# Seven half-width products of a matmul pair, with the upper and lower operand streamed in one 512-column matmul, and the lower parts of the down weights made by an accumulating transfer

## The chip, the core and the metric

The kernel runs on one core of a Trainium2 chip. The metric is the device time of one execution in microseconds, as the median of several runs. Before the change it was 2463.43 us (three runs, 2463.13 to 2463.51). In the text PE is the matmul engine (TensorE), PEld its weight loads, DVE the vector engine, ACT the scalar engine, POOL the GpSimd engine and SP the engine that issues most transfers. Every engine works through its own instructions in the order in which the program wrote them.

## The reference

Two transformer blocks on a sequence of 512 tokens with 1024 features, all in float32. What matters here are the five feed-forward networks, which hold most of the work:

```
x = x + jnp.square(jax.nn.relu(h2 @ w_up[l])) @ w_down[l]             # block 1, 4096 hidden features
...
def swiglu(h, w_gate, w_up, w_down):
    return (jax.nn.silu(h @ w_gate) * (h @ w_up)) @ w_down            # block 2, 2816 hidden, four times
```

Attention, a short convolution and the projections stand between them; the change does not touch those.

## The kernel before

**Upper and lower parts.** The fast matmul mode (float32r) keeps fewer bits than float32. So each operand is split in two: an upper part, rounded by a copy on ACT (`h`, tile `wh` for a weight), and a lower part, the rest, subtracted by DVE (`lo`, tile `wl`). A product of weights and activations is the sum of three matmuls: upper by upper, upper weights by lower activations, lower weights by upper activations. In the code these are lines 1082 to 1084, and lines 450 to 452 for ordinary tiles.

**Seven products for eight.** The weights of a hidden row come in pairs (gate and up, or two neighbouring rows of `w_up`). For most pairs the 2 by 2 block product over (weight halves, token halves) is done in the Strassen-Winograd way, with seven products of 256 columns rather than eight. `product(m, p)` does product `p` of pair `m`; `PRODUCTS = (1, 2, 6, 7, 5, 4, 3)` is the order. Each product is four K chunks by three matmuls of 256 columns. Products 1, 6, 5 and 3 accumulate one after another in the left half of a PSUM bank `X`, products 2, then 7 and 4 in the left half of a bank `YZ`; after each product ACT or DVE reads the running sum into the tiles `g` and `u`. The weight sums that products 6, 7, 5 and 3 need (`s1` to `s4`) are made by DVE in `combine` (line 355). There are 98 such pairs. The first pair or two of a network are done by `plain`, with ordinary matmuls of 512 columns.

**Stages.** `ffn_order` writes the order by hand. The hidden rows are cut in slices (four slices of 4, 6, 5 and 7 pairs in the networks of block 2, six slices in block 1). Stage 0 has the products of slice 0, after the plain pairs. Stage s holds the products of slice s and, between them, the down projection (`down`, tiles `..._D`) of slice s-1, cut in 16 items of two to four K chunks by three matmuls of 512 columns. A tail of down items of the last slice ends the network. In this text (0, ffn2) is the second network of layer 0 of block 2, and so on; `mlp` is the network of block 1.

**Weights ahead of their use.** Weights are loaded by SP in units of up to 512 KB (`raw`, five buffers) in the order of use. `split_item` (line 357) prepares one item, that is one product's or one down item's weights: ACT casts `wh` (line 376), `combine` makes the sums that the next item needs, DVE subtracts to get `wl` (line 378). `split_to` keeps five items (AHEAD) prepared beyond the one that PE works on, in a ring of seven buffers. In the written order the reading out of product i stands ahead of the preparing of item i+5, on ACT and on DVE.

**After the seventh product** `finish_relu` or `finish_silu` scales and activates `g` and `u`, and the result is split again for the down projection.

Of the kernel before, what the change touches and what calls it, by code (L numbers as in the profile page):

```python
# [231 lines left out]
def two_blocks(ctx, tc, plan, xT, wstream, vecs, sinks, rpb_g, dists, masks, outT):  # L232
# [76 lines left out]
    for i in range(4):  # L309
        s = slot[7 * i:7 * i + 7]  # L310
        lo, hi = slice(0, H), slice(H, S)
        xs.append({"b11": (s[0][:, lo], s[1][:, lo]), "t1": (s[0][:, hi], s[1][:, hi]),
                   "b21": (s[2][:, lo], s[3][:, lo]), "b22": (s[2][:, hi], s[3][:, hi]),
                   "t2": (s[4][:, lo], s[5][:, lo]), "t3": (s[4][:, hi], s[5][:, hi]),
                   "t4": (s[6][:, lo], s[6][:, hi]), "slots": s})
# [41 lines left out]
    def split_item(idx):  # L357
# [19 lines left out]
        combine(idx + 1)  # L377
        nc.vector.tensor_tensor(lo[:, :w], src, h[:, :w].bitcast(F32), ALU.subtract)  # L378
# [681 lines left out]
    def feed_forward(name, slices, pairs, start, finish, scale, prepare):  # L1060
# [6 lines left out]
        def product(m, p):  # L1067
# [363 lines left out]
```

## Time and profile before

| | |
|---|---|
| median of three runs | 2463.43 us |
| the profiled execution | 2464.76 us, span 2463.0 us |
| PE busy | 2436.1 us (99%), 15098 matmuls |
| DVE busy | 1960.7 us (80%) |
| ACT busy | 1261.0 us (51%) |
| POOL busy | 24.6 us (1%) |
| granted PE clock, mean | 0.996 (of 2.4 GHz) |

The span runs from the first to the last instruction. Busy time is the union of an engine's instructions. A matmul's duration holds its way through the array, so matmuls of one stream overlap in the records and their cost is read from start to start. The same goes, to a smaller degree, for DVE: when its instructions follow each other without a pause, each starts about 0.08 us before the one ahead of it is recorded as ended.

### The profile page before, as it was taken

Reading aid. Unit: us, or ns where it says so; the run is one execution under the profiler, and the core shown is the slowest. Engines: PE = TensorE matmul, PEld = TensorE weight load, DVE = VectorE, ACT = ScalarE, POOL = GpSimd, SP = SyncE. Lnnn points to the kernel's source line nnn. Section 1 sums busy time; section 2 is a strip of 40 time slices with the busy share of each in tenths; the row PEclk is TensorE's granted clock in tenths of the full one; section 3 lists DMA queues with packets and bytes.
Section 4 is the critical chain, followed back from the end, with each engine's and each line's share of the span. In section 5 each row is a group of like instructions: output and inputs, shape, how many; then the busy total and the mean of one; then the engine's idle time right before and its main releaser. Section 6 shows DMA issues by size and latency. Waiting matters only on the chain.

```text
span 2463.0 us, 39488 instructions
## 1 busy us (share of the span) xinstructions
PE 2436.1 (99%) x15098; PEld 2167.0 (88%) x15098; DVE 1960.7 (80%) x3943; ACT 1261.0 (51%) x2744; POOL 24.6 (1%) x37
## 2 busy tenths in 40 slices
PE   8999999999999999999999999999999999999998
PEld 6888888999879999988899999899999878999997
DVE  7778678877679878768798888898887687988885
ACT  5554355544455545544565445665445455654454
POOL 2000000000000000000000000000000000000000
PEclk9999999999999999999999999999999999999999
DMA  4222432233322332332223323323333322233332
GB/s 161 69 92 88 118 114 82 94 101 100 106 85 91 101 115 88 114 95 69 84 80 103 107 99 101 102 93 112 98 104 106 102 69 77 75 107 108 106 94 79
DMA packets 73901, 239.45 MB, mean 97 GB/s; under 512 B 8320, under 2 KB 10384, under 8 KB 73712
## 3 DMA queue, kind: packets, MB, share of 16 engines
q1 hardware_dynamic: 70496, 228.10, 29.0%
q0 software_dynamic: 1776, 7.27, 1.0%
q8 instruction: 118, 1.93, 0.3%
q10 hardware_dynamic: 1440, 1.57, 0.2%
q14 instruction: 71, 0.58, 0.1%
HBM read 234.81 MB, written 2.10 MB: 96 GB/s over the span
## 4 chain that ended last, share of the span: by engine, by line
PE 93%; DVE 5%; ACT 1%; issue 0%; DMA 0%; SPq 0%; DVEq 0%; ACTq 0%
PE X L1084 7%; PE X L1083 7%; PE X L1082 7%; PE YZ L1082 5%; PE YZ L1083 5%; PE YZ L1084 5%; PE mlp_D L451 2%; PE mlp_D L450 2%; PE mlp_D L452 2%; PE 0, 'ffn2'_D L450 2%; PE 1, 'ffn1'_D L450 2%; PE 0, 'ffn1'_D L450 2%; PE 0, 'ffn1'_D L451 2%; PE 0, 'ffn2'_D L451 2%; PE 1, 'ffn1'_D L451 2%; PE 0, 'ffn1'_D L452 2%
## 5 line engine op out<-in xcount | busy, mean ns | idle before, releaser
L378 DVE TENSOR_TENSOR wl<-raw,wh 128x512 fp32r<-128x512 f32 (+2 forms) x890 | 531.7, 609 | 98.3 <-ACT wh L376 91.4
L376 ACT CAST wh<-raw 128x512 fp32r<-128x512 f32 (+2 forms) x890 | 469.6, 555 | 8.4 <-DMA raw<-in_w 2.6
L1082 PE MATMUL X<-r,wh 128*128 128x256 f32 x1568 | 445.2, 284 | 3.8 <-ACT g L1088 3.6
L1084 PE MATMUL X<-r,wl 128*128 128x256 f32 x1568 | 444.0, 283 | 0.0
L1083 PE MATMUL X<-r,wh 128*128 128x256 f32 x1568 | 443.9, 283 | 0.0
L376 ACT CAST wh<-s 128x512 fp32r<-128x512 f32 x392 | 242.7, 620 | 224.6 <-DVE s L355 219.2
L1082 PE MATMUL YZ<-r,wh 128*128 128x256 f32 x1176 | 334.4, 284 | 0.8 <-ACT u L1094 0.8
L1083 PE MATMUL YZ<-r,wh 128*128 128x256 f32 x1176 | 333.3, 283 | 0.0
L1084 PE MATMUL YZ<-r,wl 128*128 128x256 f32 x1176 | 333.2, 283 | 0.0
L378 DVE TENSOR_TENSOR wl<-s,wh 128x512 fp32r<-128x512 f32 x392 | 268.8, 686 | 69.5 <-ACT wh L376 67.6
L1082 PEld LDWEIGHTS X<-r,wh 128*128 128x128 f32 x1568 | 300.1, 191 | 15.2 <-ACT g L1088 4.0
L1083 PEld LDWEIGHTS X<-r,wh 128*128 128x128 f32 x1568 | 300.1, 191 | 10.3 <-issue 1.2
L1084 PEld LDWEIGHTS X<-r,wl 128*128 128x128 f32 x1568 | 300.2, 191 | 0.0
L1082 PEld LDWEIGHTS YZ<-r,wh 128*128 128x128 f32 x1176 | 226.3, 192 | 1.6 <-ACT u L1094 1.4
L1083 PEld LDWEIGHTS YZ<-r,wh 128*128 128x128 f32 x1176 | 226.3, 192 | 0.2 <-issue 0.2
L1084 PEld LDWEIGHTS YZ<-r,wl 128*128 128x128 f32 x1176 | 226.3, 192 | 0.0
L1096 ACT COPY g<-X 128x256 f32<-128x256 f32 x98 | 36.5, 372 | 141.6 <-PE X L1084 141.5
L1097 DVE TENSOR_TENSOR u<-u,g 128x256 f32<-128x256 f32 x98 | 41.6, 424 | 75.8 <-ACT g L1096 75.8
L450 PE MATMUL mlp_D<-r,wh 128*128 128x512 f32 x256 | 100.1, 391 | 0.0
L451 PE MATMUL mlp_D<-r,wh 128*128 128x512 f32 x256 | 100.1, 391 | 0.0
L452 PE MATMUL mlp_D<-r,wl 128*128 128x512 f32 x256 | 99.6, 389 | 0.0
L1092 ACT COPY u<-X 128x256 f32<-128x256 f32 x98 | 36.5, 373 | 101.0 <-PE X L1084 101.0
(429 smaller groups left out, 5258.9 us busy)
## 6 DMA issues: line engine op xcount, KB each, us to landing
raw<-in_w SPq DMA_DIRECT2D x320, 512.0 KB, 3.7
raw<-in_w SPq DMA_DIRECT2D x64, 384.0 KB, 3.5
raw<-in_w SPq DMA_DIRECT2D x32, 448.0 KB, 3.5
raw<-in_w SPq DMA_DIRECT2D x32, 320.0 KB, 2.9
raw<-in_w SPq DMA_DIRECT2D x28, 256.0 KB, 2.6
bb<-in_rpb POOLq DMA_DIRECT2D x12, 384.0 KB, 3.3
xt<-in_x POOLq DMA_DIRECT2D x8, 256.0 KB, 2.9
xt<-in_x SPq DMA_DIRECT2D x1, 1024.0 KB, 12.7
```

The costliest lines, as they stand in the source:

```text
L376: nc.scalar.copy(h[:, :w], src)
L378: nc.vector.tensor_tensor(lo[:, :w], src, h[:, :w].bitcast(F32), ALU.subtract)
L450: nc.tensor.matmul(self.ps, h[:, c], hx, start=(self.n == 1), stop=False)
L451: nc.tensor.matmul(self.ps, h[:, c], lx, start=False, stop=False)
L452: nc.tensor.matmul(self.ps, lo[:, c], hx, start=False, stop=end)
L1082: nc.tensor.matmul(out, h[:, c], hx, start=first, stop=False, skip_group_check=skip)
L1083: nc.tensor.matmul(out, h[:, c], lx, start=False, stop=False, skip_group_check=skip)
L1084: nc.tensor.matmul(out, l[:, c], hx, start=False, stop=(k == 3), skip_group_check=skip)
L1092: nc.scalar.copy(u[:, lo], out)
L1096: nc.scalar.copy(g[:, hi], out)
L1097: nc.vector.tensor_tensor(u[:, hi], u[:, hi], g[:, hi], ALU.add)
```

## The change

The upper and the lower activations of a product come to stand so that one access pattern covers both: the 28 slots of 512 columns that hold them are one tile, `xall`, and the upper and the lower quarter of a product's operand lie a fixed step apart in it. Per K chunk one matmul streams 512 columns [upper, lower] against the upper weights and writes both halves of the bank; a second one streams the 256 upper columns against the lower weights into the left half. So the bank holds two partial sums, and the reading out adds them: both halves are copied or read, and more additions are done on DVE. Product 3, whose sum the finishing step read from the bank, is now read out into `g` first, and the finishing step takes `g` as one operand of 512 columns.

For down weights (`key[1:2] == ("D",)`) the lower part is no longer subtracted by DVE. ACT writes the negated upper part into `wl`, and a transfer issued by POOL adds the raw weights to it in place.

```
+    xall = cst.tile([P, 28 * S], F32R, name="xall")
...
         nc.scalar.copy(h[:, :w], src)
-        combine(idx + 1)
-        nc.vector.tensor_tensor(lo[:, :w], src, h[:, :w].bitcast(F32), ALU.subtract)
+        if key[1:2] == ("D",):
+            nc.scalar.activation(lo[:, :w], h[:, :w].bitcast(F32), AF.Copy, scale=-1.0)
+            nc.gpsimd.dma_start(lo[:, :w].bitcast(F32), src, accum_op=ALU.add)
+            combine(idx + 1)
+        else:
+            combine(idx + 1)
+            nc.vector.tensor_tensor(lo[:, :w], src, h[:, :w].bitcast(F32), ALU.subtract)
...
-                nc.tensor.matmul(out, h[:, c], hx, start=first, stop=False, skip_group_check=skip)
-                nc.tensor.matmul(out, h[:, c], lx, start=False, stop=False, skip_group_check=skip)
-                nc.tensor.matmul(out, l[:, c], hx, start=False, stop=(k == 3), skip_group_check=skip)
+                if end:
+                    nc.tensor.matmul(out, l[:, c], hx, start=False, stop=False, skip_group_check=True)
+                nc.tensor.matmul(both, h[:, c], hlx, start=first, stop=end, skip_group_check=True)
+                if not end:
+                    nc.tensor.matmul(out, l[:, c], hx, start=False, stop=False, skip_group_check=True)
             done(idx)
             g, u = d["g"], d["u"]
-            if p == 1:
-                nc.scalar.copy(g[:, lo], out)
-            elif p == 2:
-                nc.vector.tensor_tensor(g[:, lo], out, g[:, lo], ALU.add)
-            elif p == 6:
-                nc.scalar.copy(u[:, lo], out)
+            if p in (2, 4):
+                t = g if p == 2 else u
+                nc.vector.tensor_tensor(t[:, lo], out, t[:, lo], ALU.add)
+                nc.vector.tensor_tensor(t[:, lo], low, t[:, lo], ALU.add)
+            elif p in (1, 6):
+                t = g if p == 1 else u
+                nc.scalar.copy(t, d["X"])
+                nc.vector.tensor_tensor(t[:, lo], t[:, lo], t[:, hi], ALU.add)
             elif p == 7:
                 nc.scalar.copy(u[:, hi], out)
-            elif p == 5:
-                nc.scalar.copy(g[:, hi], out)
+                nc.scalar.copy(g[:, hi], low)
                 nc.vector.tensor_tensor(u[:, hi], u[:, hi], g[:, hi], ALU.add)
-            elif p == 4:
-                nc.vector.tensor_tensor(u[:, lo], out, u[:, lo], ALU.add)
             else:
-                later.extend(finish(m, g, u, out, hid))
+                t = g[:, hi]
+                nc.scalar.copy(t, out)
+                nc.vector.tensor_tensor(t, low, t, ALU.add)
+                if p == 5:
+                    nc.vector.tensor_tensor(u[:, hi], u[:, hi], g[:, hi], ALU.add)
+            if p == 3:
+                later.extend(finish(m, g, u, hid))
                 held.pop(m)
...
-            nc.vector.tensor_tensor(g[:, hi], c12, inv[:, hi], ALU.mult)
-            nc.vector.tensor_tensor(g[:, lo], g[:, lo], inv[:, lo], ALU.mult)
+    def finish_silu(m, g, u, hid):
+        nc.vector.tensor_tensor(g, g, inv, ALU.mult)
```

DVE first, in stage 2 of (0, ffn1) before the change: what stands in its queue from the reading out of product 5 of a pair to that pair's finishing step. `wl` are lower weight parts, `s` the weight sums, a name in brackets is the engine that is waited for.

```order
L1097 TENSOR_TENSOR u_9480<-u_9480,g_9479 128x256 [waits Activation_49]
L378 TENSOR_TENSOR wl_9606<-raw_9386,wh_9605 128x512 [waits PE_49,Activation_49]
L1099 TENSOR_TENSOR u_9480<-YZ_9553,u_9480 128x256 [waits PE_49]
L355 TENSOR_TENSOR s_444_9625<-raw_9441 128x512 [waits DMAHW5_49]
L355 TENSOR_TENSOR s_444_9627<-s_444_9625,raw_9386 128x512 [waits DVE_49]
L378 TENSOR_TENSOR wl_9623<-raw_9571,wh_9622 128x384 [waits DMAHW6_49,Activation_49]
L355 TENSOR_TENSOR s_445_9633<-raw_9386,raw_9441 128x512
L378 TENSOR_TENSOR wl_9631<-s_444_9627,wh_9630 128x512 [waits Activation_49]
L897 SCALAR_TENSOR_TENSOR xt<-0, 'ffn1'_D_5_9577,xt 128x512 [waits PE_49]
L1272 TENSOR_TENSOR g_9479<-X_9478,inv 128x256 [waits PE_49]
L1273 TENSOR_TENSOR g_9479<-g_9479,inv 128x256
L1274 TENSOR_TENSOR u_9480<-u_9480,inv 128x512
```

The same part of DVE's queue for a pair of that network with the change.

```order
L1118 TENSOR_TENSOR g_9563<-X_9562,g_9563 128x256 [waits Activation_49]
L1120 TENSOR_TENSOR u_9564<-u_9564,g_9563 128x256 [waits DVE_49]
L391 TENSOR_TENSOR wl_9660<-raw_9481,wh_9659 128x512 [waits Activation_49]
L1105 TENSOR_TENSOR u_9564<-YZ_9632,u_9564 128x256 [waits PE_49]
L1106 TENSOR_TENSOR u_9564<-YZ_9632,u_9564 128x256 [waits DVE_49]
L362 TENSOR_TENSOR s_473_9678<-raw_9483 128x512 [waits DMAHW7_49]
L362 TENSOR_TENSOR s_473_9680<-s_473_9678,raw_9481 128x512 [waits DVE_49]
L362 TENSOR_TENSOR s_474_9685<-raw_9481,raw_9483 128x512
L391 TENSOR_TENSOR wl_9683<-s_473_9680,wh_9682 128x512 [waits Activation_49]
L910 SCALAR_TENSOR_TENSOR xt<-0, 'ffn1'_D_1_9596,xt 128x512 [waits PE_49]
L1118 TENSOR_TENSOR g_9563<-X_9562,g_9563 128x256 [waits Activation_49]
L1284 TENSOR_TENSOR g_9563<-g_9563,inv 128x512 [waits DVE_49]
```

The down item's subtraction (128x384) is gone; products 5, 4 and 3 have one more addition each, and three of the added or widened instructions wait for the one just ahead of them on DVE.

PE, before: the start of product 3 of a pair, which accumulates in `X` after product 5.

```order
L1082 MATMUL X_9478<-r_90,wh_9567 128x256 [waits Activation_49]
L1083 MATMUL X_9478<-r_91,wh_9567 128x256
L1084 MATMUL X_9478<-r_90,wl_9568 128x256
L1082 MATMUL X_9478<-r_97,wh_9567 128x256
L1083 MATMUL X_9478<-r_98,wh_9567 128x256
L1084 MATMUL X_9478<-r_97,wl_9568 128x256
```

PE, with the change: the end of a down item of three K chunks, and then the start of product 3 of a pair.

```order
L465 MATMUL 0, 'ffn1'_D_4_9021<-r_7186,wl_8943 128x512
L1098 MATMUL X_8881<-xall,wh_8961 128x512 [waits DVE_49]
L1100 MATMUL X_8881<-xall,wl_8962 128x256
L1098 MATMUL X_8881<-xall,wh_8961 128x512
L1100 MATMUL X_8881<-xall,wl_8962 128x256
L1098 MATMUL X_8881<-xall,wh_8961 128x512
```

Three matmuls of 256 columns have become one of 512 and one of 256; and product 3 now waits for DVE, which reads product 5's lower half out of the bank, where it waited for ACT alone.

ACT, with the change, in stage 3 of (0, ffn1): around a down item, whose `wl` is written by the second of its two rows and added to by a transfer.

```order
L1117 COPY g_9867<-X_9866 128x256 [waits PE_49]
L383 CAST wh_10025<-raw_9780 128x384
L386 ACTIVATE wl_10026<-wh_10025 128x384 [waits DMASW4_49,Activation_49]
L1109 COPY g_10033<-X_10032 128x512 [waits PE_49]
L1290 ACTIVATE g_9867<-g_9867 128x512 [waits DVE_49]
```

Between the cast and PE's use of `wl` there now stand an ACT instruction, a POOL instruction and a transfer, where there was one DVE instruction.

## Rows read from the trace of the kernel before

**Rows 1.** The page: busy time by engine, and the chain that ended last.
```profile
PE 2436.1 (99%) x15098; PEld 2167.0 (88%) x15098; DVE 1960.7 (80%) x3943; ACT 1261.0 (51%) x2744; POOL 24.6 (1%) x37
PE 93%; DVE 5%; ACT 1%; issue 0%; DMA 0%; SPq 0%; DVEq 0%; ACTq 0%
```

**Rows 2.** Timeline of PE (start us, us long): a product, then a down item.
```profile
1366.96 0.28 PE L1082 MATMUL YZ<-r,wh 128*128 128x256 f32 x1
...
1368.29 0.28 PE L1084 MATMUL YZ<-r,wl 128*128 128x256 f32 x1
1368.41 0.40 PE L450 MATMUL 0, 'ffn2'_D<-r,wh 128*128 128x512 f32 x1
...
1370.47 0.28 PE L1082 MATMUL X<-r,wh 128*128 128x256 f32 x1
```

**Rows 3.** Busy us by window: stages 0 to 3 of (0, ffn2).
```profile
1250.50:1283.00 32.50, 32.26 (x264) 31.55 (x263) 31.27 (x59) 21.18 (x42) 0.00 (x0) 1.00 0.26 90
1283.00:1365.50 82.50, 82.50 (x602) 78.39 (x601) 73.47 (x140) 44.55 (x95) 0.00 (x0) 1.00 0.32 103
1365.50:1448.90 83.40, 83.40 (x567) 77.44 (x566) 67.23 (x122) 39.59 (x82) 0.00 (x0) 1.00 0.31 102
1448.90:1546.90 98.00, 98.00 (x710) 92.96 (x709) 83.16 (x154) 51.36 (x108) 0.00 (x0) 1.00 0.33 105
```

**Rows 4.** The same view: stages 0 and 1 of (0, ffn1).
```profile
736.40:763.50 27.10, 23.74 (x172) 22.38 (x171) 26.62 (x47) 15.20 (x31) 0.00 (x0) 0.94 0.21 68
763.50:846.10 82.60, 82.60 (x603) 78.49 (x602) 74.38 (x142) 44.63 (x96) 0.00 (x0) 1.00 0.33 103
```

**Rows 5.** Timeline of DVE in stage 0 of (0, ffn2).
```profile
1274.40 0.41 DVE L1272 TENSOR_TENSOR g<-X,inv 128x256 f32<-128x256 f32 x1
1274.74 0.41 DVE L1273 TENSOR_TENSOR g<-g,inv 128x256 f32<-128x256 f32 x1
1275.07 0.68 DVE L1274 TENSOR_TENSOR u<-u,inv 128x512 f32<-128x512 f32 x1
1275.67 0.68 DVE L378 TENSOR_TENSOR wl<-s,wh 128x512 fp32r<-128x512 f32 x1
...
1280.39 0.68 DVE L355 TENSOR_TENSOR s<-raw 128x512 f32<-128x512 f32 x1
1281.11 0.69 DVE L355 TENSOR_TENSOR s<-s,raw 128x512 f32<-128x512 f32 x1
```

**Rows 6.** Groups by line and shape: DVE's subtractions of 256 and 384 columns.
```profile
L378 DVE TENSOR_TENSOR wl<-raw,wh 128x384 fp32r<-128x384 f32 x192 | 105.3, 553 | 32.3 <-ACT wh L376 32.3
L378 DVE TENSOR_TENSOR wl<-raw,wh 128x256 fp32r<-128x256 f32 x160 | 66.3, 418 | 11.0 <-ACT wh L376 10.5
```

**Rows 7.** Windows: the third product stage of the `mlp` network.
```profile
430.73:482.91 52.18, 52.18 (x351) 48.22 (x350) 42.41 (x81) 27.28 (x61) 0.00 (x0) 1.00 0.31 99
```

**Rows 8.** Timeline of ACT: the cast of a down item's weights.
```profile
1288.93 0.40 ACT L376 CAST wh<-raw 128x256 fp32r<-128x256 f32 x1
1289.24 0.36 ACT L1094 COPY u<-YZ 128x256 f32<-128x256 f32 x1
```

**Rows 9.** Timeline of PE: the first use of the same item's weights.
```profile
1292.99 0.40 PE L450 MATMUL 0, 'ffn2'_D<-r,wh 128*128 128x512 f32 x1
...
1293.45 0.39 PE L452 MATMUL 0, 'ffn2'_D<-r,wl 128*128 128x512 f32 x1
```

**Rows 10.** The page, transfers: count, KB each, median us from issue to landing.
```profile
bb<-in_rpb POOLq DMA_DIRECT2D x12, 384.0 KB, 3.3
xt<-in_x POOLq DMA_DIRECT2D x8, 256.0 KB, 2.9
...
out<-xt ACTq DMA_DIRECT2D x8, 128.0 KB, 1.8
...
dst<-in_dist POOLq DMA_DIRECT2D x1, 320.0 KB, 8.8
```

**Rows 11.** The page's groups: casts of weights, idle time before them, and what ended it.
```profile
L376 ACT CAST wh<-raw 128x512 fp32r<-128x512 f32 (+2 forms) x890 | 469.6, 555 | 8.4 <-DMA raw<-in_w 2.6
```

More of the change, by code (lines that the diff above doesn't have):

```diff
@@ L251, in two_blocks @@
     whole, slot = [None] * 52, [None] * 52
+    xall = cst.tile([P, 28 * S], F32R, name="xall")
     def use_slot(i, dtype):
+        if i < 28:
+            assert dtype == F32R
+            whole[i] = slot[i] = xall[:, S * i:S * i + S]
+            return slot[i]
         whole[i] = slot_p.tile([P, S if i < 50 else 768], dtype, tag=f"r{i}", name=f"r{i}")
@@ L310, in two_blocks @@
         s = slot[7 * i:7 * i + 7]
[L311 to L315, printed above, removed]
+        quarters = xall[:, 7 * i * S:7 * i * S + 7 * S].rearrange("p (a q) -> p a q", q=H)
+        xs.append({name: (quarters[:, k:k + step + 1:step, :], quarters[:, k, :])
+                   for name, k, step in (("b11", 0, 2), ("t1", 1, 2), ("b21", 4, 2), ("b22", 5, 2),
+                                         ("t2", 8, 2), ("t3", 9, 2), ("t4", 12, 1))})
+        xs[i]["slots"] = s
     st = {"unit": 0, "split": 0, "next": 0, "off": 0}
@@ L1072, in product @@
             if p in (2, 7):
-                d["YZ"] = bank(f"YZ{m}")[:, :H]
-            out = d["YZ"] if p in (2, 7, 4) else d["X"][:, :H]
+                d["YZ"] = bank(f"YZ{m}")
+            both = d["YZ"] if p in (2, 7, 4) else d["X"]
+            out, low = both[:, :H], both[:, H:]
+            both = both.rearrange("p (a q) -> p a q", a=2)
             idx = item(key, p, 0)
@@ L1077, in product @@
             for k in range(4):
-                hx, lx = xs[k][A_OF[p]]
+                hlx, hx = xs[k][A_OF[p]]
                 c = slice(P * k, P * k + P)
-                first = k == 0 and p in (1, 2, 7)
-                skip = p not in (1, 2, 7)
-                nc.tensor.matmul(out, h[:, c], hx, start=first, stop=False, skip_group_check=skip)
-                nc.tensor.matmul(out, h[:, c], lx, start=False, stop=False, skip_group_check=skip)
-                nc.tensor.matmul(out, l[:, c], hx, start=False, stop=(k == 3), skip_group_check=skip)
+                first, end = k == 0 and p in (1, 2, 7), k == 3
@@ L1131, in plain_end @@
             (_, t0, i0), (_, t1, i1) = held.pop(m)
-            later.extend(finish(m, t0, t1, None, hid))
+            later.extend(finish(m, t0, t1, hid))
             later.append(lambda: give(i0 + i1))
@@ L1249, in feed_forward, with finish_relu @@
         return first, rest
-    def finish_relu(m, g, u, c12, hid):
-        lo, hi = slice(0, H), slice(H, S)
-        if c12 is None:
-            nc.vector.scalar_tensor_tensor(g, g, 0.0, inv, ALU.max, ALU.mult)
-        else:
-            nc.vector.scalar_tensor_tensor(g[:, hi], c12, 0.0, inv[:, hi], ALU.max, ALU.mult)
-            nc.vector.scalar_tensor_tensor(g[:, lo], g[:, lo], 0.0, inv[:, lo], ALU.max, ALU.mult)
+    def finish_relu(m, g, u, hid):
+        nc.vector.scalar_tensor_tensor(g, g, 0.0, inv, ALU.max, ALU.mult)
         nc.vector.scalar_tensor_tensor(u, u, 0.0, inv, ALU.max, ALU.mult)
@@ L1265, in finish_relu @@
         return [lambda: split(m, g), lambda: split(m + 1, u)]
-    def finish_silu(m, g, u, c12, hid):
-        lo, hi = slice(0, H), slice(H, S)
-        if c12 is None:
-            nc.vector.tensor_tensor(g, g, inv, ALU.mult)
-        else:
-            nc.vector.tensor_tensor(g[:, hi], c12, inv[:, hi], ALU.mult)
-            nc.vector.tensor_tensor(g[:, lo], g[:, lo], inv[:, lo], ALU.mult)
+    def finish_silu(m, g, u, hid):
+        nc.vector.tensor_tensor(g, g, inv, ALU.mult)
         nc.vector.tensor_tensor(u, u, inv, ALU.mult)
```

## The prediction

> **What bounds the kernel now.** I read four views in this order. First the page: PE is busy 99% of the span and holds 93% of the chain that ended last, while DVE is busy 80% and ACT 51% [rows 1]. So PE is the bound on the whole, and DVE is the engine with the least to spare. Second the timeline of PE, for the price of a matmul from start to start: the twelve 256-column matmuls of a product take 1368.41 - 1366.96 = 1.45 us, 0.120 us each, and the nine 512-column ones of a down item 1370.47 - 1368.41 = 2.06 us, 0.229 us each. A 256-column one behind a 512-column one and a 512-column one behind a 256-column one go at the same prices, by the width of the one ahead [rows 2]. Third, windows laid on the stages of one network, since 80% is a mean: DVE is busy 31.27 of 32.50 us in stage 0 (96%), 73.47 of 82.50 in stage 1 (89%), 67.23 of 83.40 in stage 2 (81%), 83.16 of 98.00 in stage 3 (85%) [rows 3]. In (0, ffn1) stage 0 has 26.62 of 27.10 [rows 4]. Stage 0 has products alone, and there DVE is a second bound already. Fourth DVE's own timeline in that stage: its rows follow without a pause, so the step from start to start is the price: 0.34 us for 256 columns, 0.60 for 512, and 0.72 where the next instruction needs the result of this one (1280.39 to 1281.11), 0.12 more [rows 5].
>
> **The change, part by part.**
>
> *Matmuls.* A K chunk cost 3 x 0.120 = 0.360 us and will cost 0.229 + 0.120 = 0.349 us. There are 98 pairs x 7 products x 4 chunks = 2744 chunks, so 2744 x 0.011 = 30 us of PE time go, 0.31 us per pair. A third of the weight loads of these products goes with them, but the loads lie beside the matmuls (PEld is busy 88% under PE's 99% [rows 1]). This is the largest gain that the change can have. A price for 512 columns split in two runs of 256 in memory is not in the trace; the nearest rows bound the chunk by 0.349 and, if two runs cost as two matmuls, 0.360. I take the first.
>
> Against the row stands a rule of the Trainium skill, "TensorE: Matmul & The Clock Gate", section "Back-to-back issue gap": at full clock a matmul takes its columns divided by 2.4 GHz plus about 2.5 ns, so merging two would save 2.5 ns, an estimate of 6.9 us over 2744 chunks and not 30. The trace does not agree with it here: the rule gives 109 ns and 216 ns where the rows have 120 and 229.
>
> *Reading out, on DVE.* Gone per pair are five 256-column instructions (L1090, L1097, L1099, L1272, L1273). New are ten of 256 columns and one of 512: two each for products 2 and 4, one each for 1, 6, 7 and 3, two for 5, and the finishing step on `g` at full width. That is 5 x 0.334 + 0.60 = 2.27 us more. Four of them wait for the instruction ahead of them on DVE (the second additions of 2 and 4, the one behind product 5's, the finishing step behind product 3's): 4 x 0.12 = 0.48 us. Together 2.75 us per pair, 270 us over 98 pairs. If the waits cost nothing it is 2.27.
>
> *Down weights, off DVE.* Each of the 352 down items drops one subtraction: 0.34 us at 256 columns, 0.47 at 384 (the means of 418 and 553 ns less the overlap of 0.08 us, 0.68 against a step of 0.60), 0.60 at 512 [rows 5, 6]. Of these items 128 have 256 columns, 192 have 384 and 32 have 512, by the code: 128 x 0.34 + 192 x 0.47 + 32 x 0.60 = 153 us, but they fall in stages 1 to 3 and the tails. None falls in stage 0.
>
> *By stage.* For (0, ffn2), which the two networks of layer 1 resemble, stages 0 and 1 have three and six pairs and stage 1 has 16 down items of 256 columns. DVE: 31.27 + 73.47 - 16 x 0.34 + 9 x 2.75 = 124.1 us, where the two stages take 115.0 us now and PE would need 115.0 - 9 x 0.31 = 112.2. DVE becomes the bound. How far may it lag? Weights are prepared five items ahead, but product 3 starts when DVE has read product 5's lower half out of the same bank, and in stage 0 only product 4 (1.4 us) stands between. So I give DVE 1 us of lag, and the two stages take 123 us: 8 us more. (0, ffn1) has two pairs in stage 0: 26.62 + 74.38 - 5.4 + 8 x 2.75 = 117.6 us against 109.7, less the same 1 us: 7 more. Over the four networks 3 x 8 + 7 = 31 us lost.
> Stage 2 holds 16 down items of 384 columns: DVE 67.23 - 16 x 0.47 + 5 x 2.75 = 73.5 us against PE's 83.4 - 5 x 0.31 = 81.9. PE bounds: 1.5 us gained, 6 over four networks.
> Stage 3 holds eight of 256 and eight of 384 columns: DVE 83.16 - 8 x 0.34 - 8 x 0.47 + 7 x 2.75 = 95.9 us, PE 98.0 - 7 x 0.31 = 95.8. A tie; two queues that wait on each other lose a little, so 97 and 1 us gained, 4 over four networks.
> `mlp` has many down items to a pair: DVE 42.41 of 52.18 us for three pairs [rows 7], and 42.41 + 3 x 2.75 - 16 x 0.34 = 45.2 stays under PE's 51. Fifteen pairs gain 15 x 0.31 = 4.6; its one pair without down items has 2.75 us more on DVE, of which the lag takes most, and loses about 1: 3.6 gained.
>
> *Down weights, by ACT and the transfer.* ACT gets 352 negations of some 0.4 us (the nearest rows are its cast and copy of 256 columns, 0.40 and 0.36 [rows 8]) and wider copies. It is busy 21.18 of 32.50 us at most [rows 3], so throughput is no issue; latency is. The item of stage 1 with the shortest notice is cast at 1288.93, its `wh` is used at 1292.99 and its `wl` first at 1293.45: 4.5 us [rows 8, 9]. The new way takes the cast 0.40, a negation of 0.40, and a transfer from POOL. No row shows an accumulating transfer. POOL's plain ones land after 2.9 us for 256 KB and 3.3 for 384; the shortest of any is 1.8 and the longest of POOL's 8.8, in the first microseconds beside the opening loads [rows 10]. Most down items move 128 or 192 KB. I take 2.9, the nearest row: 0.4 + 0.4 + 0.1 + 2.9 = 3.8 us, within 4.5, cost nothing. At 1.8 it is nothing too; at 8.8 it would be late by some 5 us on each of the 272 items that lie between products. The cover is gone at a landing of about 3.6 us. Behind a late `wl` stands all of PE's queue. On POOL nothing else is queued in these networks. On SP the load that refills a `raw` buffer now waits for the transfer that reads it, some 3 us later than for DVE; casts waited 2.6 us in all for loads [rows 11], and five buffers are ahead, so this costs nothing as long as a buffer's turn (about 4 us for 512 KB of weights) times five exceeds the load and the added 3 us.
>
> *Sum.* 31 - 6 - 4 - 3.6 = +17 us on the profiled execution's 2464.76 us, 1.3 us over the median of the runs. On the median: 2481 us.
>
> **The rivals.** *DVE's additions hide and PE's gain stays.* DVE is 80% busy over the span [rows 1], some 500 us free for a net 117 of new work (270 - 153), and five prepared items are 7 us of lead. If the lag is allowed to be that, if no own wait costs anything (9 x 2.27 rather than 9 x 2.75), stages 0 and 1 come to 119.8 - 5 = 115 us, even with now, and stages 2 and 3 give 1.5 + 2.2 each: 4 x 3.7 + 3.6 = 18 us gained, 2445 us; with everything hidden 2433. Against it: DVE runs without a pause through stage 0 already [rows 5], and the wait in front of product 3 cuts the lead. It decides if DVE's work in stages 0 and 1 stays under about 116 us.
> *The transfers are late.* If adding in place doubles what a transfer does, a landing near 4.5 us, the short-notice items are late by up to 1 us. With 272 items between products, a third to a half of them late, and a part of it under DVE's own lag, that is 50 us: 2530 us. For it: nothing in the trace shows that kind of transfer, and the raw loads keep the transfer engines 32% busy [rows 3]. Against: the size is below that of the 2.9 us row.
> *Merging saves less.* With 2.5 ns a chunk in place of 11, stages 2 and 3 and `mlp` lose their gain, 13.6 us down to about 1: 2494 us. The rule of the skill's page on TensorE named above would have it so.
> That the change does not do what it says I rule out: 2744 matmuls are gone from PE's queue, and the attention and projection stages keep their waits, though 28 slots are one tile.
>
> **How the numbers follow.** DVE-bound stages 0 and 1, as summed: 0.52, from 2460 to 2508 (3% of idle DVE time in stages 0, 1 and 3 would add 27 us to 2481; 2.27 a pair takes 16 from it and a little more lag the rest). Hidden additions: 0.20, 2433 to 2458. Late transfers: 0.23, 2490 and far up. Merging that saves little: 0.05. The predicted time is 2481 us. The range 2448 to 2530 leaves out about half of the second case and a third of the third. A measurement of this kernel tells 0.2% from no change, about 5 us: faster 0.20, the same 0.08 (the near end of the first case), slower 0.72.
>
> **What would show it.** PE: in products, steps of 0.229 and 0.120 us. DVE busy near 100% in stages 0 and 1 of the block 2 networks and about 98% in stage 3, with PE idle in front of product 3 put down to DVE's reading of `X`; stage 0 of (0, ffn2) near 39 us and stage 1 near 84; stage 2 near 82 and set by PE. Transfers from POOL landing under 3.6 us, and no idle PE in front of a down item's third matmul. I am wrong if PE waits there on transfers, or if stages 0 and 1 together come to 115 us or less.

## The result, and the profile after

The changed kernel takes 2660.38 us (median of four runs, 2651.63 to 2665.0), the kernel before 2463.47 (2463.13 to 2464.25) beside it. The ratio is 1.0795, with a 95% interval of 1.0766 to 1.0823: 197 us slower, where 17 were forecast. The direction was right, the size was not, and the time lies outside the range.

The profiled execution took 2651.63 us, with a span of 2649.9 us and a mean granted clock of 0.980 (0.996 before). These lines of its page answer to [rows 1, 10]: busy times, the software queue, the chain, and the transfers of `wl` (count, KB each, median us to landing).

```profile
PE 2486.7 (94%) x12354; PEld 2038.7 (77%) x12354; DVE 2074.7 (78%) x4179; ACT 1524.8 (58%) x3292; POOL 332.4 (13%) x389
...
q0 software_dynamic: 52464, 70.20, 15.9%
...
PE 56%; DMA 14%; issue 14%; DVE 12%; ACT 4%; POOL 1%; POOLq 0%; SPq 0%; DVEq 0%; ACTq 0%
...
wl<-raw POOLq DMA_DIRECT2D x192, 192.0 KB, 3.9
...
wl<-raw POOLq DMA_DIRECT2D x128, 128.0 KB, 2.8
...
wl<-raw POOLq DMA_DIRECT2D x32, 256.0 KB, 5.1
```

DMA held 0% of the chain before; now 14% of the span is chained to it, and 13% is `DMA wl<-raw` alone. DVE's share of the span fell from 80 to 78%, so the kernel is not simply DVE-bound. The medians of landing are 2.8 to 5.1 us, where the prediction took 2.9 for all. The median hides the worse part: over the 352 transfers a tenth land after 6.3 us or later, the latest after 7.8.

Who stands still is in the waits of PE over the whole span (us in total, times, the longest):

```profile
PE 0, 'ffn2'_D L465 <- DMA wl<-raw: 23.1, 13, 3.4
PE 1, 'ffn2'_D L465 <- DMA wl<-raw: 22.2, 14, 3.8
PE mlp_D L465 <- DMA wl<-raw: 21.6, 21, 3.1
PE 1, 'ffn1'_D L465 <- DMA wl<-raw: 19.6, 12, 3.7
PE 0, 'ffn1'_D L465 <- DMA wl<-raw: 18.9, 11, 3.4
```

L465 is the third matmul of a down item, the first that reads `wl`. It waits 71 times, 105.4 us in all. One of these waits on PE's timeline, in stage 2 of (0, ffn2), with the merged products ahead of it; the first three lines answer to [rows 2]:

```profile
1463.82 0.40 PE L1098 MATMUL X<-xall,wh 128*128 128x512 f32 x1
1464.06 0.28 PE L1100 MATMUL X<-xall,wl 128*128 128x256 f32 x1
1464.18 0.40 PE L1098 MATMUL X<-xall,wh 128*128 128x512 f32 x1
...
1466.86 0.40 PE L464 MATMUL 0, 'ffn2'_D<-r,wh 128*128 128x512 f32 x1
1469.77 0.50 PE L465 MATMUL 0, 'ffn2'_D<-r,wl 128*128 128x512 f32 x1 [2.51 <-DMA wl<-raw]
...
1472.09 0.63 PE L1098 MATMUL X<-xall,wh 128*128 128x512 f32 x1
1472.51 0.41 PE L1100 MATMUL X<-xall,wl 128*128 128x256 f32 x1
1472.72 0.63 PE L1098 MATMUL X<-xall,wh 128*128 128x512 f32 x1
```

A chunk takes 1464.18 - 1463.82 = 0.36 us before the wait and 1472.72 - 1472.09 = 0.63 after it. PE idled 2.5 us, and about 1 us after it resumed the clock dropped to the lower level (1.2 GHz), for 3.4 us. So this wait is paid twice. It is not so for all: behind 14 of the 71 waits, 1.9 to 3.8 us long, the clock fell within 1.5 us after PE had resumed, each time for 3.4 us; behind the other 57, 0.2 to 3.7 us long, it did not. The granted clock sums it up, as an estimate: (1 - 0.980) x 2650 = 53 us of PE's speed lost, against (1 - 0.996) x 2463 = 10 before. Of the 53 us, 14 x 3.4 / 2 = 24 lie right behind such waits.

Why was this transfer late? POOL's timeline, and the transfers of the stretch from 1462 to 1470 us (issues, KB, median us to landing):

```profile
1462.66 0.87 POOL L387 DMA_DIRECT2D wl<-raw  x1 [2.74 <-ACT wl L386]
```

```profile
raw<-in_w SPq DMA_DIRECT2D x2, 512.0 KB, 4.9
raw<-in_w SPq DMA_DIRECT2D x1, 384.0 KB, 4.5
wl<-raw POOLq DMA_DIRECT2D x2, 192.0 KB, 5.1
```

Three loads of raw weights were issued from 1462.20 to 1463.10 us, around the transfer's issue at 1462.66. It landed after 7.1 us; the one issued at 1467.59, when most of these loads were done, after 3.1.

The windows of (0, ffn2) answer to [rows 3] (busy us of PE, PEld, DVE, ACT, POOL with counts; clock, DMA share, GB/s):

```profile
1320.29:1360.55 40.26, 33.05 (x179) 26.82 (x178) 39.20 (x76) 24.17 (x48) 0.00 (x0) 1.00 0.20 72
1360.55:1454.05 93.50, 86.66 (x433) 72.43 (x432) 83.34 (x159) 56.02 (x123) 14.83 (x17) 0.95 0.45 113
1454.05:1544.86 90.81, 85.08 (x425) 70.61 (x424) 74.09 (x138) 52.20 (x107) 13.08 (x15) 0.98 0.51 128
1544.86:1658.43 113.57, 102.56 (x514) 85.68 (x513) 93.34 (x176) 66.79 (x141) 17.44 (x20) 0.95 0.45 113
```

Two different losses. Stage 0 has no transfer and grew from 32.5 to 40.3 us with DVE busy 97%: that one was forecast (near 39). Stages 1 to 3 grew by 11, 7 and 16 us with DVE at 82 to 89% and the clock under 1: that one was not. In stage 0 PE waits for the reading out, and for nothing else:

```profile
PE X L1098 <- DVE g L1118: 2.4, 2, 1.4
PE X L1098 <- ACT u L1109: 2.1, 2, 1.4
PE YZ L1098 <- ACT g L1113: 1.8, 2, 0.9
PE X L1098 <- ACT g L1109: 0.9, 1, 0.9
```

### The profile page after: what moved, and what is told of

It reads as the page before. It is cut to its first block, busy times and chain, and to the rows that moved or that the text cites. A ratio compares the mean times of both kernels' runs of the same rounds, so it can differ in the third digit from the quotient of the medians.

```text
span 2649.9 us, 35945 instructions
## 1 busy us (share of the span) xinstructions
PE 2486.7 (94%) x12354; PEld 2038.7 (77%) x12354; DVE 2074.7 (78%) x4179; ACT 1524.8 (58%) x3292; POOL 332.4 (13%) x389
## 4 chain that ended last, share of the span: by engine, by line
PE 56%; DMA 14%; issue 14%; DVE 12%; ACT 4%; POOL 1%; POOLq 0%; SPq 0%; DVEq 0%; ACTq 0%
DMA wl<-raw 13%; PE X L1098 6%; PE YZ L1098 3%; DVE wl L391 3%; PE X L1100 2%; DVE s L362 2%; PE 0, 'ffn1'_D L465 1%; PE 1, 'ffn1'_D L465 1%; PE 0, 'ffn2'_D L465 1%; PE YZ L1100 1%; PE 1, 'ffn2'_D L465 1%; PE 0, 'ffn1'_D L463 1%; PE 0, 'ffn1'_D L464 1%; ACT wh L383 1%; PE 1, 'ffn1'_D L463 1%
## 5 line engine op out<-in xcount | busy, mean ns | idle before, releaser
L1098 PE MATMUL X<-xall,wh 128*128 128x512 f32 x1568 | 596.4, 411 | 27.5 <-DVE g L1118 10.7
L387 POOL DMA_DIRECT2D wl<-raw x352 | 307.5, 879 | 1990.9 <-ACT wl L386 854.4
L1098 PE MATMUL YZ<-xall,wh 128*128 128x512 f32 x1176 | 440.4, 396 | 8.4 <-ACT g L1113 8.4
L391 DVE TENSOR_TENSOR wl<-raw,wh 128x512 fp32r<-128x512 f32 (+1 forms) x538 | 354.5, 670 | 30.4 <-ACT wh L383 28.7
L1098 PEld LDWEIGHTS X<-xall,wh 128*128 128x128 f32 x1568 | 300.8, 196 | 86.7 <-DVE g L1118 15.4
L1100 PE MATMUL X<-xall,wl 128*128 128x256 f32 x1176 | 339.1, 288 | 0.0
L1098 PEld LDWEIGHTS YZ<-xall,wh 128*128 128x128 f32 x1176 | 222.0, 189 | 38.6 <-ACT g L1113 12.1
L1100 PE MATMUL YZ<-xall,wl 128*128 128x256 f32 x882 | 248.2, 281 | 0.0
L1100 PEld LDWEIGHTS X<-xall,wl 128*128 128x128 f32 x1176 | 231.9, 197 | 17.3 <-issue 0.5
L386 ACT ACTIVATE wl<-wh 128x256 fp32r<-128x256 f32 (+2 forms) x352 | 174.7, 496 | 11.2
L465 PE MATMUL mlp_D<-r,wl 128*128 128x512 f32 x256 | 103.7, 405 | 21.8 <-DMA wl<-raw 21.6
L1097 PE MATMUL X<-xall,wl 128*128 128x256 f32 x392 | 111.6, 285 | 0.0
L465 PE MATMUL 0, 'ffn2'_D<-r,wl 128*128 128x512 f32 x176 | 72.0, 409 | 23.3 <-DMA wl<-raw 23.1
L465 PE MATMUL 1, 'ffn1'_D<-r,wl 128*128 128x512 f32 x176 | 71.9, 408 | 19.6 <-DMA wl<-raw 19.6
```

The source lines that it names most:

```text
L386: nc.scalar.activation(lo[:, :w], h[:, :w].bitcast(F32), AF.Copy, scale=-1.0)
L387: nc.gpsimd.dma_start(lo[:, :w].bitcast(F32), src, accum_op=ALU.add)
L465: nc.tensor.matmul(self.ps, lo[:, c], hx, start=False, stop=end)
L1097: nc.tensor.matmul(out, l[:, c], hx, start=False, stop=False, skip_group_check=True)
L1098: nc.tensor.matmul(both, h[:, c], hlx, start=first, stop=end, skip_group_check=True)
L1100: nc.tensor.matmul(out, l[:, c], hx, start=False, stop=False, skip_group_check=True)
```

## The experiments

All times are medians beside runs of the kernel before on the same chip (2463.6 to 2464.0 us).

### e1 and e2: each half of the change alone

e1 keeps the merged products and gives the down weights back to DVE:

```
-        if key[1:2] == ("D",):
-            nc.scalar.activation(lo[:, :w], h[:, :w].bitcast(F32), AF.Copy, scale=-1.0)
-            nc.gpsimd.dma_start(lo[:, :w].bitcast(F32), src, accum_op=ALU.add)
...
+        combine(idx + 1)
+        nc.vector.tensor_tensor(lo[:, :w], src, h[:, :w].bitcast(F32), ALU.subtract)
```

> The changed kernel with the lower down weights subtracted on DVE again; the merged products stay. Theory L (the transfers are what lost most of the 197 us: they land late beside the raw loads and hold the raw blocks): no transfer is left, and what remains is DVE's added reading-out, 2.75 us a pair. From the stages of the profile before: stage 0 of each network 7.6 us longer as in the changed kernel, stages 0 and 1 together 31.27 + 73.47 + 9 x 2.75 = 129.5 on DVE against 115.0 us, with 1 us of lag 13.5 us lost (12.3 in (0, ffn1)), stage 2 even, stage 3 DVE 83.2 + 7 x 2.75 = 102.4 against 98.1, 4.3 lost, mlp 3 gained: 2463 + 3 x 13.5 + 12.3 + 4 x 4.3 - 3 = 2530 us, 2500 to 2545. Theory M (the merged products are what loses, by PE's waits before products 3 and 7, and the transfers only show beside them): 2580 us or more, and stages 1 to 3 at least as long as in the changed kernel (93.5, 90.8, 113.6 us in (0, ffn2)).

e2 puts the removed lines into the kernel before.

> The kernel before with only the lower down weights made by the copy with the sign turned and the accumulating transfer; products as before, three matmuls a chunk. Theory L: stage 0, which has no down items, keeps its 32.5 us; stages 1 to 3 and mlp's lose by late transfers some 8 to 14 us each as in the changed kernel, 17 stages x about 9 us = 150, so 2590 to 2640 us; landing median 3.5 us or more, and PE stands before third matmuls of down items for about 100 us. Theory M: the transfers hide, DVE has 153 us less, 2445 to 2475 us.

Measured: e1 2536.27 us (ratio 1.0293, 1.0276 to 1.0311), e2 2544.55 (1.0328, 1.0312 to 1.0343). Theory L holds for e1 in size and, but for `mlp`, in place: the product stages of `mlp` lost 4.7 us where 3 gained were expected. Its windows of (0, ffn2):

```profile
1274.08:1314.34 40.26, 33.05 (x179) 26.82 (x178) 39.20 (x76) 24.16 (x48) 0.00 (x0) 1.00 0.21 72
1314.34:1401.41 87.07, 83.92 (x433) 68.75 (x432) 85.87 (x173) 48.34 (x106) 0.00 (x0) 1.00 0.30 97
1401.41:1483.87 82.46, 82.31 (x425) 69.77 (x424) 79.67 (x154) 44.77 (x92) 0.00 (x0) 1.00 0.32 103
1483.87:1586.43 102.56, 97.89 (x514) 82.32 (x512) 100.29 (x198) 57.06 (x121) 0.00 (x0) 1.00 0.31 97
```

Stages 0, 1 and 3 are DVE's (39.20 of 40.26, 85.87 of 87.07, 100.29 of 102.56 us busy), stage 2 is PE's. In e2 stage 0 keeps its 32.45 us and PE waits 54.8 us for `wl`; 81 us were lost where about 150 were expected. Each half loses 72 to 81 us alone, the two together 197: in the merged kernel the same transfers cost PE 105 us of waiting, not 55. There they have less notice: a tenth of them have at most 3.3 us from their issue to the moment when PE is ready for them, in e2 4.0. What shortens it stays open; from the cast to the issue both kernels take 1.35 us (median).

### e3: a plain transfer

```
-            nc.gpsimd.dma_start(lo[:, :w].bitcast(F32), src, accum_op=ALU.add)
+            nc.gpsimd.dma_start(lo[:, :w].bitcast(F32), src)
```

> The changed kernel with a plain transfer raw to wl where it adds into wl (the subtraction is left out, so the lower parts of the down weights are wrong). Same instructions, queues and waits. Theory A (adding in place is what makes a transfer long): landing falls to about 2.0 to 2.5 us by the median, the waits before third matmuls go, and the time comes near 2500 us. Theory L (the raw loads beside them and the held raw blocks): median landing stays at 3.3 us or more with a tail of 6 to 7, and the time stays above 2600 us.

### e4: the same transfer from a tile that is not `raw`

```
-            nc.gpsimd.dma_start(lo[:, :w].bitcast(F32), src, accum_op=ALU.add)
+            nc.gpsimd.dma_start(lo[:, :w].bitcast(F32), h[:, :w].bitcast(F32), accum_op=ALU.add)
```

> The changed kernel, but each transfer adds from wh, the copy that ACT has made, in place of the raw block (so the lower parts of the down weights come out as zero). Size, queue and the moment of issue are the same; raw blocks are free as soon as ACT has read them. Theory H (the held raw blocks are the larger part of L: loads are released in bursts and run into the next transfers): bursts go, median landing about 3.0 us with few above 5, raw loads come early, and the time falls to 2500 to 2550 us. Theory C (the transfers share the queues with the raw loads whatever releases these): median landing 3.6 us or more and 2600 us or more.

Measured: e3 2542.63 us (1.0321, 1.0306 to 1.0337), e4 2678.6 (1.087, 1.0853 to 1.0886). The landings on the page of e3 and then of e4:

```profile
wl<-raw POOLq DMA_DIRECT2D x192, 192.0 KB, 2.8
...
wl<-raw POOLq DMA_DIRECT2D x128, 128.0 KB, 2.1
...
wl<-raw POOLq DMA_DIRECT2D x32, 256.0 KB, 3.6
```

```profile
wl<-wh POOLq DMA_DIRECT2D x192, 192.0 KB, 4.7
...
wl<-wh POOLq DMA_DIRECT2D x128, 128.0 KB, 3.7
...
wl<-wh POOLq DMA_DIRECT2D x32, 256.0 KB, 5.2
```

e3 gives theory A most of what it asked: without the adding, 118 us come back and PE's waits for `wl` shrink from 105 to 34 us, though the median landing over all sizes is 2.7 us, not 2.0 to 2.5, and the time not near 2500. e4 refutes theory H: with the raw blocks free early the loads come earlier, 186 of the 352 transfers have two or more of them beside (128 in the changed kernel), landings get longer and the kernel 18 us slower. So it is both the adding and the company. Counted from the traces (a load is beside a transfer when it is issued 0.5 us or more before the landing and lands 1.5 us or more after the transfer's issue):

| raw loads beside | changed kernel: count, median us | e3, plain: count, median us |
|---|---|---|
| 0 | 100, 2.97 | 132, 2.11 |
| 1 | 124, 3.76 | 128, 3.37 |
| 2 | 86, 5.02 | 66, 3.90 |
| 3 or more | 42, 6.51 | 26, 4.67 |

A long landing meets more loads by itself, so the table alone would prove little; e4 shows the direction. Two other causes do not show in the changed kernel. A transfer issued before the one ahead of it on POOL's queue has landed is no later for that: with one load beside 3.76 us against 3.75, with two 5.01 against 5.03. And DVE's work does not hold them up: with no load beside, nine tenths of the 50 transfers of 192 KB land after 2.95 to 3.30 us, in a kernel whose DVE is busy 78% of the span. The fit of the Trainium skill, "DMA: Bandwidth & Descriptors", section "Anatomy of one DMA — SWDGE (gpsimd) path", gives 2.0 us + bytes / 436 KB per us, for 192 KB an estimate of 2.5 us. The plain ones come near it when alone (median 2.13 us at this size); the adding ones stay above it (3.01), and no run has one of any size under 2.6.

### e8: one item more of notice

```
-AHEAD = 5
+AHEAD = 6
```

> The changed kernel with its weights prepared six items ahead in place of five, in the same seven buffers. Theory L: a down item of 384 columns takes PE 2.1 us, so the transfers get about 2 us more; landings of 4 to 6 us come in time, PE's waits before third matmuls (some 106 us) fall to under 50, and the time to 2560 to 2600 us. Theory R (the raw loads arrive too late for any look-ahead, since they wait for transfers): within 15 us of 2652.

Measured: 2524.52 us (1.0246, 1.0232 to 1.026), 136 us less than the changed kernel and better than either theory had it. The transfers land about as before (3.5, 3.0 and 5.1 us by size). What is left of PE's waits for them:

```profile
PE mlp_D L465 <- DMA wl<-raw: 1.5, 2, 1.0
PE 1, 'ffn2'_D L465 <- DMA wl<-raw: 0.4, 1, 0.4
PE 0, 'ffn2'_D L465 <- DMA wl<-raw: 0.4, 1, 0.4
```

2.3 us against 105.4. A tenth of the transfers had at most 3.7 us from issue to first use before (PE's wait included), now at most 4.8. Idle time and clock explain the gain between the two profiled executions (spans of 2649.9 and 2524.1 us). 103 us of these waits go, PE's waits for ACT and DVE grow by 22 (from 50.7 to 72.2), and the granted clock, back at 0.995, returns 53 - 13 = 40 us: 121 of the 126 us.

### e9 to e11: what is left

e9 is e8 with the pairs of each first stage as in the kernel before (`single` holds these pairs; the old body runs for them). e10 is e2 with `AHEAD = 6`, e11 the kernel before with `AHEAD = 6`.

> The kernel of e8 (look-ahead six, transfers and merged products) with the pairs of each network's first stage multiplied and read out as in the kernel before. Theory D (what e8 still loses is stage 0, by DVE's added reading-out, and it ends there): stage 0 back at 32.5 us (27.1 in (0, ffn1)) and 3 x 7.7 + 6.6 = 30 us less than e8's 2524.5, so 2495 us, 2488 to 2502. Theory C (DVE's lag is handed on, so stage 1 loses what stage 0 gets back): 2510 us or more.

> The kernel of e2 (transfers alone, products as before) with look-ahead six. Theory N (the transfers lose only by their short notice): PE's 55 us before third matmuls go as in e8, the stages return to before's, and the time to 2460 to 2472 us. Theory X (the transfers also cost otherwise, by ACT's turned copies or the shared queues): 2485 us or more.

> The kernel before with look-ahead six, nothing else. Control for e8 and e10. Theory N: the notice is spare for DVE's subtraction, so within 0.2% of 2463.5 us. Rival: a longer look-ahead gives by itself, 2455 us or less, or costs by itself (ACT waits on a buffer that PE still reads), 2470 us or more.

Measured: e9 2495.48 us (1.0128, 1.0114 to 1.0142), e10 2472.65 (1.0034, 1.0021 to 1.0048), e11 2466.81 (1.0014, 1.0004 to 1.0023). e9 and e11 came as the first theory had it, e10 just over its upper end. With these the 197 us can be laid out as steps, in this order, each the difference of two kernels:

| step | us |
|---|---|
| transfers with too short a notice (changed kernel to e8) | 135.9 |
| merged products in the first stages (e8 to e9) | 29.0 |
| merged products in the other stages, and the one tile `xall` (e9 to e10) | 22.8 |
| transfers that have their notice (e10 to e11) | 5.8 |
| the longer look-ahead (e11 to before, 2463.8) | 3.0 |

The third step mixes two things, since e10 has the separate slots of the kernel before: the one tile alone gains 15.8 us (e13 below), and if it does so in e9 too, the merging itself loses more than 22.8 there.

### e5 to e7: POOL in place of the transfer

```
-            nc.scalar.activation(lo[:, :w], h[:, :w].bitcast(F32), AF.Copy, scale=-1.0)
-            nc.gpsimd.dma_start(lo[:, :w].bitcast(F32), src, accum_op=ALU.add)
+            nc.gpsimd.tensor_tensor(lo[:, :w], src, h[:, :w].bitcast(F32), ALU.subtract)
```

> The changed kernel with the lower down weights subtracted on POOL (one instruction; no turned copy, no transfer). DVE and PE keep what the changed kernel gives them. This is the sum of the prediction without transfers. Theory S (what is left without the transfers is stage 0's DVE and little else): stage 0 at 40.3 us, 30 lost over four networks; stage 1 87.1 of e1 less 16 x 0.34 on DVE, 82 to 84; stage 2 82; stage 3 96 to 98; mlp 2 to 3 us over before; about 2485 us, 2470 to 2500. Theory P (POOL's subtraction is late for PE as the transfer was, or slows DVE beside it): stage 1 stays at 87 us or more, and 2520 us or more.

e6 also moves the additions that touch no bank (`t[:, lo] + t[:, hi]`, `u[:, hi] + g[:, hi]`) from `nc.vector` to `nc.gpsimd`; e7 is e6 with unmerged first stages.

> As e5, and also the four additions a pair that touch no bank (behind products 1, 6, 7 and 5) on POOL in place of DVE: 4 x 0.33 us and their waits off DVE's row. Theory S: stage 0 shrinks by about 4 us from 40.3 (three pairs by 1.3 to 1.5), product 3 still waits for DVE's reading of product 5; stages 1 to 3 come to PE's 81, 82, 96: about 2465 us, 2455 to 2478. Theory P: POOL takes longer than DVE for them and DVE then waits for POOL before products 2 and 4 are read: stage 0 no shorter, 2490 us or more.

> As e6, but the pairs of each network's first stage are multiplied and read out as in the kernel before (three matmuls a chunk). Theory S: stage 0 back at 32.5 us, the others at PE's pace: the merged chunks' 9 ns show, 2440 to 2455 us, faster than the kernel before. Theory P: stages 1 to 3 longer than before, 2475 us or more.

Measured: e5 2585.59 us (1.0493, 1.0479 to 1.0508), e6 2562.2 (1.0398, 1.0384 to 1.0412), e7 2524.96 (1.0246, 1.0232 to 1.026). Theory S failed three times, by 70 to 86 us beyond its upper end. e5 is 49 us slower than e1, although DVE has 352 instructions fewer. Its DVE is busy 2176 us where the changed kernel's, with the same instructions, has 2075. The lines of DVE say which got longer (ns: minimum, median, maximum), first in the changed kernel, then in e5:

```profile
L362 DVE TENSOR_TENSOR s<-raw x98: 681/682/689, 373.9 to 2581.1; 128x512 f32<-128x512 f32 x98
```

```profile
L362 DVE TENSOR_TENSOR s<-raw x98: 679/682/1501, 374.2 to 2517.3; 128x512 f32<-128x512 f32 x98
...
L1117 DVE TENSOR_TENSOR g<-X,g x196: 408/418/425, 388.0 to 2534.7; 128x256 f32<-128x256 f32 x196
```

An addition of two SBUF tiles takes up to 1.5 us when POOL's subtraction (1.1 us by the mean) runs beside it; the one that reads a bank (`X`) keeps its 0.42. Over the whole trace 214 instructions of DVE are more than 0.05 us longer than the median of their kind in the changed kernel, 119 us in all. Every one of them runs beside a POOL subtraction, and of 271 that read a bank beside one, none is longer. PE itself never waits for POOL in e5. The Trainium skill, "SBUF — State Buffer", section "SBUF: two separate sides", states that DVE and GpSimd share one pair of ports, held for a whole instruction by whoever comes first, and that a DVE instruction with two SBUF inputs needs it. The trace agrees: the addition of 1.50 us above began 0.52 us after the start of a POOL subtraction of 1.47 us and ended 0.55 us after its end. My expectation treated POOL as free. In e6 392 additions more went to POOL and stage 0 of (0, ffn2) stayed at 41.0 us, no shorter than the 40.3 of e1, as theory P had it; e7 only takes the first stages out of the loss.

### e12 to e15: what the merging itself gives

e12 is the kernel before with merged products in the third stages and in `mlp`'s last three; `single` holds all other pairs. In e1 these stages were shorter than before, but for the first of the three of `mlp` (63.82 us, before 63.06). Unlike the kernel before, e12 has its operands in the one tile.

> The kernel before, with the products merged only in the stages where e1 was shorter than before: the third stage of each of the four networks and mlp's last three stages (29 of 98 pairs); lower weights on DVE, look-ahead five, all else as before. Theory D (merging pays where PE bounds with DVE's room beside it): 4 x 0.87 + 3 x 0.78 = 5.8 us gained, 2457 us, 2455 to 2460. Rival (the stages that follow pay DVE's lag back): 2463 us or more.

Measured: 2449.13 us (0.9939, 0.9927 to 0.9952), faster than either side had it: the stages that were *not* merged got shorter too, 82.56 to 81.06 and 98.08 to 96.33 us in (0, ffn2). Their steps are 117 ns (before 120). All that differs for them is that the 28 operand slots are one tile. e13 keeps that alone:

```
+    xall = cst.tile([P, 28 * S], F32R, name="xall")
...
     def use_slot(i, dtype):
+        if i < 28:
+            assert dtype == F32R
+            whole[i] = slot[i] = xall[:, S * i:S * i + S]
+            return slot[i]
```

> The kernel before with the 28 operand slots in one tile as in the changed kernel, and nothing merged. Theory A (the steps are shorter because the operand lies elsewhere: the slots begin at an address that is a multiple of 64 bytes, before 32 off one): 256-column steps of 117 ns, stages 1, 2 and 3 at 81.0, 82.1 and 96.3 us, 512-column steps from these slots 233 ns; 2449 us, 2446 to 2452, as fast as e12. Theory M (the merged stages of e12 gave by being merged): those 29 pairs lose 7.6 us again, 2456 us or more.

e14 has the separate slots of the kernel before, moved by 32 bytes; e15 is e12 with the one tile's slots moved by 32 bytes.

```
     for i in range(52):
+        if i in (0, 28):
+            slot_p.tile([P, 8], F32, tag=f"pad{i}", name=f"pad{i}")
         use_slot(i, F32R)
```

```
-    xall = cst.tile([P, 28 * S], F32R, name="xall")
+    xall = cst.tile([P, 28 * S + 16], F32R, name="xall")[:, 8:28 * S + 8]
```

> The kernel before with 32 bytes ahead of its first slot and 32 behind its 28th: the 28 operand slots, separate tiles as before, begin at multiples of 64 bytes, all other tiles where they were modulo 64. Theory A: same as e13, 2449 us, 2446 to 2452, 256-column steps of 117 ns. Theory T (one tile, and what follows for waits between instructions, makes the difference): steps of 120 ns and within 0.2% of 2463.5 us.

> The kernel of e12 with the one tile's slots moved by 32 bytes, so that they lie 32 off a multiple of 64 as in the kernel before. Theory A: 256-column steps 120 ns and 512-column steps 227 ns again; unmerged stages back at 82.56 and 98.08 us, a merged chunk 347 ns in place of 360: third stages 81.5, mlp's last three 62.0; 2463.5 - 4 x 1.8 - 3 x 1.1 = 2453 us, 2451 to 2456. Theory T: as e12, 2449 us or less, with steps of 117 and 233.

Measured: e13 2447.83 us (0.9935, 0.9922 to 0.9947), e14 2460.73 (0.9987, 0.9978 to 0.9997), e15 2456.8 (0.9971, 0.9961 to 0.9982). The windows of (0, ffn2) in e13, and the third stage of e12, the merged one:

```profile
1245.49:1277.83 32.34, 31.81 (x263) 30.92 (x262) 31.04 (x58) 21.09 (x42) 0.00 (x0) 1.00 0.27 90
1277.83:1358.89 81.06, 81.06 (x602) 76.92 (x601) 73.34 (x140) 44.56 (x95) 0.00 (x0) 1.00 0.33 105
1358.89:1440.93 82.04, 82.04 (x566) 76.06 (x565) 67.14 (x122) 39.57 (x82) 0.00 (x0) 1.00 0.33 104
1440.93:1537.16 96.23, 96.23 (x711) 91.17 (x709) 83.17 (x154) 51.42 (x108) 0.00 (x0) 1.00 0.35 107
```

```profile
1360.51:1442.53 82.02, 82.02 (x426) 69.83 (x425) 77.70 (x151) 44.07 (x90) 0.00 (x0) 1.00 0.32 104
```

82.02 us merged and 82.04 unmerged, from the same tile: there merging gives nothing, for 10.6 us more of DVE. The timeline of PE in e13 shows the step, a product in 1300.25 - 1298.85 = 1.40 us where [rows 2] had 1.45:

```profile
1298.85 0.28 PE L1088 MATMUL X<-xall,wh 128*128 128x256 f32 x1
...
1300.25 0.28 PE L1088 MATMUL YZ<-xall,wh 128*128 128x256 f32 x1
```

| where the operand slots lie | 256-column step, ns | unmerged chunk | merged chunk |
|---|---|---|---|
| 32 bytes off a multiple of 64 (before, e15) | 120 | 360 | 350 (234.5 + 115.5) |
| one tile from a multiple of 64 (e12, e13) | 117 | 351 | 351 (233.5 + 117.5) |

Theory A holds for e13 and, for the unmerged steps, e15. A merged chunk costs the same at either place, where e15 expected 347 ns. So from the place of the old slots merging does gain, as the third stage of (0, ffn2) in e15 shows:

```profile
1361.35:1443.46 82.11, 82.11 (x426) 69.98 (x425) 77.70 (x151) 44.03 (x90) 0.00 (x0) 1.00 0.32 104
```

It took 83.34 us before: 1.23 us for 140 chunks, 8.8 ns each, and `mlp`'s last three stages give the same 8.8 (62.32 us, before 63.06, 84 chunks). Merging alone and the move alone each take 9 to 10 ns off a chunk, and the two together no more.

e14 is between: the median step is 117 ns, but 18% take 122 or more, and the time falls by 2.9 us and not by 14. So the address matters (e12 and e15 differ by 32 bytes and nothing else), and 64 bytes are not the whole rule. What else decides stays open. No trace holds an address: the moves by 32 bytes are in the edits, the multiples of 64 are the expectations' reckoning.

## Why the prediction was wrong

**The failed step** is the transfer: "I take 2.9, the nearest row: 0.4 + 0.4 + 0.1 + 2.9 = 3.8 us, within 4.5, cost nothing." The landing is the term that was mis-sized most. The row had a plain transfer; the new ones add in place (2.97 us in place of 2.11 alone) and go out beside the raw loads, and with each further load the median is 0.8 to 1.5 us longer. The prediction named its own limit, "gone at a landing of about 3.6 us", and the median was 3.8. The way to the issue was short as well: from the start of the cast to the issue lie 1.35 us by the median where 0.9 were taken, so cast and transfer together take 5.2 us, and a tenth of them 7.7 or more. And 4.5 us was the shortest notice of (0, ffn2), not of the kernel: before the change five items of `mlp` and three of (0, ffn1) have 3.2 to 4.4. Cost: 136 us by e8, not 0.

**The rival had the mechanism and a third of the size.** Late transfers at 50 us took a landing near 4.5 us and a third to a half of 272 items late by up to 1 us. Fewer were late, 71, but by more: the true loss comes from the tail, up to 7.8 us, which leaves PE idle for up to 3.8 us at a time, with a lower clock behind the longer waits: 105 us idle and some 40 us of speed.

**The raw buffers**, which now wait for the transfers, were put at nothing, and e4 bears it out: freeing them sooner did not help.

**DVE's additions** were right in size on DVE and a quarter short in what they cost. DVE's busy time rose by 114 us, forecast 270 - 153 = 117. With transfers in time (e8) stages 0 and 1 lost 42 us over four networks, forecast 31; stage 2 gained 4.8, forecast 6.

**Stage 3 and `mlp`** were mis-sized: 3.1 to 3.4 us lost in each stage 3 of e8 (forecast 1 gained) and 7.7 in `mlp` (forecast 3.6 gained). DVE was not full in stage 3 of e8, 92.47 of 101.44 us; PE waited for single reads. Summing an engine's work over a stage is too kind where each read stands between two products. The rest of the 43 us between 2481 and e8's 2524.5 is 10.9 us in stages 0 and 1, 1.2 in stage 2, and about 4 outside the networks' stages (5 in e13), where 512-column steps from the moved slots take 233 ns (before 227).

**The merging's gain** of 11 ns a chunk was 9 in the trace, and right for the slots of the kernel before: 10 ns by e15 (350 ns, before 360). But the edit also moved the slots, and from the one tile an unmerged chunk takes 351 ns as well (e13), so the merged products of the changed kernel give nothing that the move would not have given without them. The rule that the prediction cited from the Trainium skill, "TensorE: Matmul & The Clock Gate", section "Back-to-back issue gap", stated there for an isolated matmul, would have it 2.5 ns; the runs show 10 at the one place and about 0 at the other (a step of 233.5 against two of 117). So the rival "merging saves less" is false at the old place and true from the tile that came with the change.

**The layout** had no term at all in the prediction. It is the part of the change worth keeping: e13, 15.8 us (0.65%) faster than the kernel before and the shortest time here, with e12 1.3 us behind.

## What to carry to other kernels

Price a new transfer by the load beside it, and compare the tail of its landing, not the median, with the shortest notice of its reader; an item more of look-ahead is cheap to try and told more here than any other run. When an edit moves data as well as instructions, run the move alone: here it gave 15.8 us, with nothing left for the merging to add. Work moved to POOL is not free for DVE instructions that read two tiles of SBUF beside it.

## What the hardware showed that I had not expected

- Behind a PE wait of 2.5 us came a stretch of 3.4 us at the lower clock, a chunk of 0.63 us in place of 0.36; so it was behind 14 of the 71 waits for `wl`.
- An accumulating transfer keeps POOL 0.87 us in its issue (a plain one 0.54) and takes 2.97 us alone (median over the sizes; plain 2.11), 6.5 with three loads or more beside it.
- The step of a matmul depends on where its operand lies: 120 or 117 ns for 256 columns, and the other way round 227 or 233 for 512. Two runs of 256 in one matmul took 234 to 235 at either place.
- DVE instructions with two SBUF inputs took up to 1.5 us in place of 0.68 beside POOL, those that read a bank did not.
